# The gated MLP's up-projections as Strassen block products, and its down-projection in pairs of row tiles

## The chip, the core and the metric

The kernel runs on one core of a Trainium2 chip. The metric is device microseconds (us) of one execution. TensorE (PE) does the matmuls and loads their weights (PEld); VectorE (DVE), ScalarE (ACT) and GpSimd (POOL) do the elementwise work; SyncE (SP) and, for a few transfers, ACT and POOL issue DMAs. Each engine takes its instructions in the order in which they stand in its queue; an instruction that waits holds up all behind it. Products accumulate in PSUM, in eight banks of 128 partitions x 512 float32.

## The reference, cut to what matters

One layer of a bidirectional encoder: x is 1024 positions by 1024 model dimensions in float32. Two branches (latent attention and a two-way linear recurrence) are gated, merged by `w_merge` and added to x. What the change touches is what comes then:

```python
x = x + (gates[:, :, 0] * y_a + gates[:, :, 1] * y_b) @ w_merge[l]
h = rms_norm(x, norm_ffn_g[l])
gp = dwconv_centered(h @ w_ffn_gate[l], ffn_conv_w[l], ffn_conv_b[l])   # 3 taps along the positions
x = x + (jax.nn.silu(gp) * (h @ w_ffn_up[l])) @ w_ffn_down[l]
```

`w_ffn_gate` and `w_ffn_up` are 1024 x 2816 and `w_ffn_down` is 2816 x 1024; `rms_norm` divides each position by the root of its mean square and multiplies by the gain `norm_ffn_g`.

## The kernel before, in words

Everything lies transposed: 128 features (or model dimensions) on the partitions, 1024 positions along the free axis, in two halves of 512 (`HT`). A float32 product is made of three passes: each operand is the sum of a high and a low part (`split`: ACT casts the high part, L163; POOL or DVE subtracts it for the low part, L164), and the products high-high, high-low and low-high are added in PSUM. A **pass** here is one matmul of a 128 x 128 weight block with 128 x 512 of the operand.

Phase A is the input projection with its gates; the gates (`gt`) are written to DRAM (`d_gate`). Phase B runs attention and the recurrence, its work on PE ordered by a planner. Phase C, from 1276 us, forms the second branch's product, adds it to the first branch's (`y0`, loaded from DRAM as 512 KB per tile), splits the sum into `yx`, multiplies by `w_merge` (`product(two_, a["w_merge"][j], yx)`), and adds the residual, which gives `x2`, eight tiles j of 128 model dimensions. From each tile come the operands of phase D: `h2h` and `h2l`, the high and low parts of x2 times the gain (L1488 on ACT, L1489 on DVE), and its squares (L1493 on ACT), which POOL adds up (L1494). The residual is not divided by its rms: the product's evacuation multiplies by `rs2`, one over the rms of each position.

Phase D, from 1394 us, is the gated MLP in 22 tiles of 128 features, taken in four groups (`GROUPS`, 6, 6, 5 and 5 tiles). Of each tile, `product` first does the gate half (`w_fg`, 8 row blocks x 2 halves x 3 = 48 passes), then the up half (`w_fu`, 48). DVE evacuates the gate half times `rs2` (L1517), ACT and DVE do the convolution's three taps (L1522, L1523, L1524), ACT applies Silu (L121, in `act`), POOL multiplies by `rs2` (L1527), DVE multiplies with the up half from PSUM (L1528) and splits into `sh` and `sl` (L163, L164). After a group comes its share of the down product: for each of eight output tiles, group size x 2 halves x 3 passes into two banks, which DVE adds onto `x2` (L1535). In the last group each tile is then stored as 512 KB (L1537). The four pairs of banks take turns, so the evacuation of one product lies beside the passes of the next.

SBUF pools lie on two sides. `hp`, on the right, holds the first operands of the projection, and later those of phase D (`place("hh0", ...)` and so on: a tile in the place of an earlier operand). `yq`, `xp2`, `fp` and the weights' pool lie on the left. Weights come in pieces of 128 x 512 float32, 256 KB, through two places (`wraw`, then `whi` and `wlo`), issued by SP.

## Time and profile before

| | us |
|---|---|
| runs | 2135.06, 2125.6, 2127.84 (median 2127.84) |
| span of the profiled execution | 2126.6 |
| PE busy in it | 1958.1 (92%) |
| DVE, ACT, POOL busy | 997.4, 843.1, 871.8 (47%, 40%, 41%) |
| phase C | from 1276 to 1394.2 |
| phase D's matmuls | 1394.2 to 2121.4 |

The profiled execution's span lies 1.2 us under the median of the runs. Several views of the trace are used below. In a table of time windows each row has the window and its length, then the busy time of PE, PEld, DVE, ACT and POOL, each with its count of instructions, then PEclk, the clock that the throttle granted to PE as a share of full speed, then the mean busy share of the 16 DMA engines and GB/s. A row of the groups of instructions names line, engine, operation, output and inputs (`b<-h2h,whi`: bank b from operand h2h and weights whi), shape, count; behind the first bar stand its busy time in total (us) and the mean of one (ns); behind the second the engine's idle time just before these instructions and what ended it. A row of the timeline has start, duration, engine and instruction, with the idle time before it and its releaser in brackets.

### The profile page before, as it was taken

What the parts mean: (1) busy time and instruction counts of PE and PEld (TensorE: products, weight loads), DVE (VectorE), ACT (ScalarE), POOL (GpSimd) and SP (SyncE); (2) the same over time, 40 slices, a digit from 0 to 9 for tenths busy, and PEclk for the clock granted to TensorE, in tenths of its full rate; (3) what the DMA queues carried; (4) which work ended last, traced back from release to release, by engine and by line L of the source; (5) the groups of instructions that cost most, each with busy time, mean ns of one, the idle gap of its engine ahead of it and who ended that gap; (6) DMA issues with size and microseconds to landing.
All of it is one profiled execution on the core that took longest, in us unless ns stands there. A gap on an engine that the chain in (4) does not pass through costs nothing.

```text
span 2126.6 us, 31745 instructions
## 1 busy us (share of the span) xinstructions
PE 1958.1 (92%) x12280; PEld 1507.2 (71%) x12280; DVE 997.4 (47%) x1560; ACT 843.1 (40%) x1459; POOL 871.8 (41%) x763
## 2 busy tenths in 40 slices
PE   7799999899898779888779999999999999999999
...
GB/s 144 34 140 230 145 162 219 104 145 113 98 130 125 78 108 106 104 135 79 100 86 91 205 303 189 50 45 50 43 53 50 50 43 52 50 39 56 50 38 117
DMA packets 212551, 221.09 MB, mean 104 GB/s; under 512 B 114152, under 2 KB 138792, under 8 KB 212400
## 3 DMA queue, kind: packets, MB, share of 16 engines
...
## 4 chain that ended last, share of the span: by engine, by line
PE 51%; DVE 7%; DMA 3%; issue 1%; SPq 1%; POOL 0%; ACT 0%; DVEq 0%; POOLq 0%; ACTq 0%
PE b L251 13%; PE b L248 13%; PE b L249 13%; DMA IN<-dn 2%; DVE Ti L815 2%; DVE tm L811 2%; DVE mx L1151 1%; PE po L1179 1%; PE st L1205 1%; PE po L1181 1%; PE st L1207 1%; PE po L1180 1%; PE st L1206 1%; PE ct L972 1%; PE st L248 1%
## 5 line engine op out<-in xcount | busy, mean ns | idle before, releaser
L164 POOL TENSOR_TENSOR wlo<-wraw,whi 128x512 fp32r<-128x512 f32 x248 | 306.8, 1240 | 792.6 <-ACT whi L163 788.7
L163 ACT CAST whi<-wraw 128x512 fp32r<-128x512 f32 x248 | 145.2, 586 | 652.4 <-PE b L249 462.1
L248 PE MATMUL b<-h2h,whi 128*128 128x512 f32 x704 | 274.3, 390 | 0.0
L249 PE MATMUL b<-h2l,whi 128*128 128x512 f32 x704 | 273.9, 389 | 0.0
L1217 POOL TENSOR_TENSOR pl<-pe,ph 128x512 fp32r<-128x512 f32 x128 | 169.6, 1327 | 131.2 <-ACT ph L1216 128.6
L251 PE MATMUL b<-h2h,wlo 128*128 128x512 f32 x704 | 216.7, 389 | 0.0
L248 PE MATMUL st<-hh,whi 128*128 128x512 f32 x408 | 176.0, 431 | 15.2 <-ACT hh L275 9.0
L249 PE MATMUL st<-hl,whi 128*128 128x512 f32 x408 | 164.7, 404 | 0.5 <-DVE hl L276 0.5
L248 PEld LDWEIGHTS b<-h2h,whi 128*128 128x128 f32 x704 | 132.2, 188 | 27.7 <-issue 0.2
L249 PEld LDWEIGHTS b<-h2l,whi 128*128 128x128 f32 x704 | 132.2, 188 | 27.7 <-issue 0.2
L251 PEld LDWEIGHTS b<-h2h,wlo 128*128 128x128 f32 x704 | 132.2, 188 | 27.5
L251 PE MATMUL st<-hh,wlo 128*128 128x512 f32 x408 | 140.9, 400 | 0.5 <-POOL wlo L164 0.5
L248 PE MATMUL b<-sh,whi 128*128 128x512 f32 x352 | 138.8, 394 | 0.0
L249 PE MATMUL b<-sl,whi 128*128 128x512 f32 x352 | 138.7, 394 | 0.0
L1535 DVE TENSOR_TENSOR x<-b,x 128x1024 f32<-128x1024 f32 x32 | 39.2, 1225 | 197.6 <-PE b L251 197.6
L811 DVE TENSOR_TENSOR tm<-IN,Ti 128x126 f32<-128x126 f32 (+22 forms) x248 | 91.2, 368 | 77.5 <-DMA IN<-dn 71.3
L251 PE MATMUL b<-sh,wlo 128*128 128x512 f32 x352 | 110.4, 394 | 0.0
L248 PEld LDWEIGHTS st<-hh,whi 128*128 128x128 f32 x408 | 79.6, 195 | 43.0 <-issue 9.8
L815 DVE TENSOR_TENSOR Ti<-Ti,tm 128x126 f32<-128x126 f32 (+22 forms) x248 | 104.3, 421 | 6.6
L1517 DVE TENSOR_TENSOR u<-b,rs 128x1024 f32<-128x1024 f32 x22 | 26.9, 1224 | 169.6 <-PE b L251 158.4
L1216 ACT CAST ph<-pe 128x512 fp32r<-128x512 f32 x128 | 79.1, 620 | 64.5 <-PE po L1181 61.3
L980 POOL TENSOR_TENSOR sm<-RR,pcs 64x128 f32<-64x128 f32 x112 | 47.6, 425 | 126.4 <-DVE RR L1002 105.2
...
## 6 DMA issues: line engine op xcount, KB each, us to landing
...
```

Of the source, the lines that this page charges most:

```text
L163: S.copy(hi, x)
L164: (eng or G).tensor_tensor(out=lo, in0=x, in1=hi.bitcast(F32), op=sub)
L248: nc.tensor.matmul(o, wh, xh[:, hs], start=first, stop=False)
L249: nc.tensor.matmul(o, wh, xl[:, hs], start=False, stop=False)
L251: nc.tensor.matmul(o, wl, xh[:, hs], start=False, stop=last)
L811: t = V.tensor_tensor(out=tm[:, 0:nt, 0:nj], in0=IN[:, s, s + 1:32][:, :, None].to_broadcast([128, nt, nj]), in1=Ti[:, s, 0:nj][:, None, : ...
L815: V.tensor_tensor(out=Ti[:, s + 1:32, 0:nj], in0=Ti[:, s + 1:32, 0:nj], in1=tm[:, 0:nt, 0:nj], op=add)
L980: state["pool"] = G.tensor_tensor(out=sm[hs], in0=RR[hs, :, h, 0, :], in1=pcv[hs, i // 4, :, i % 4, None].to_broadcast([64, 2, C]), op=mult)
L1216: S.copy(ph, pe)
L1217: G.tensor_tensor(out=pl, in0=pe, in1=ph.bitcast(F32), op=sub)
L1517: V.tensor_tensor(out=u, in0=pg, in1=rs2, op=mult)
L1535: V.tensor_tensor(out=x2[:, j, :], in0=ps, in1=x2[:, j, :], op=add)
```

## The change

**The operands.** The two up-projections of a feature tile are taken as one product of 2 x 2 blocks. The weights' blocks are A11 and A12 (the halves of `w_fu`'s model dimensions, 0 to 511 and 512 to 1023) and A21 and A22 (of `w_fg`). The operand's are B11 and B12 (dimensions 0 to 511, first and second half of the positions) and B21 and B22 (dimensions 512 to 1023). Strassen's scheme in Winograd's form needs seven products of such blocks where eight stood, here called **one** to **seven**, each of 4 row blocks x 3 = 12 passes into one bank (`quarter`):

| product | weights | operand | bank |
|---|---|---|---|
| one | A11 | B11 | ba |
| two | A12 | B21 | ba, added to one |
| three | s2' = A12 - s2 | B22 | bc, added to five |
| four | A22 | T4 = B21 - T2 | bb, added to six and seven |
| five | s1 = A21 + A22 | T1 = B12 - B11 | bc |
| six | s2 = s1 - A11 | T2 = B11 + T3 | bb |
| seven | A21' = A11 - A21 | T3 = B22 - B12 | bb, added to six |

In the code T1 to T4 are `U1` to `U4`, with tiles named t1h, t1l and so on. T1, T2 and T3 are made in phase C with the tiles j of x2: for j < 4 B11 and T1 (with a subtraction on POOL), for j >= 4 B21, B22, T3 and T2, each with its high and low part. T4 is made at the beginning of phase D, on DVE with ACT's casts (`u2` is its intermediate there). B11, T1, B21 and B22 lie in `hp`, in the places of the earlier h2h and h2l; T2 and T3 lie in a new left-hand pool `bq` (whose places hold y0 and gt before), T4 in `fp`.

**A feature tile.** Four weight blocks are loaded into six places in turn (`raw_`), POOL makes s1, s2, A21' and s2' from them, each is split on ACT and DVE into one of three pairs of places in turn (`parts_`; the down weights' low parts are POOL's). The order on PE is one, six, the down share, five, seven, two, four, three; in the first tile it is one, five, the sums of squares, two, six, seven, four, three. Between them DVE adds bank contents: p1 is a copy of one's bank (ACT), u2 = six + p1, u3 = six and seven + p1; bc + u3 and bb + p1 (after four) give the second and first half of the gate, each multiplied by rs2 into `u`; bc + u2 after three gives the up half's second part. The convolution and Silu follow, then per half the product with the up half in place in PSUM (L1665), and the split into sh (ACT, L1666) and sl (DVE, L1667). The up half is not multiplied by `rs2` any more.

**The residual.** x2 is multiplied after the first tile by the rms itself (`irs`, eight multiplies of 128 x 1024 on POOL, L1670), the down products are added to it, and each half tile is multiplied by rs2 at the very end (DVE, L1697) and stored as 256 KB.

**The down product** goes by pairs of row tiles (2 k blocks) instead of groups of 5 or 6: 16 units of 6 passes, one bank each (three banks `dbank` in turn; the up-projections have five, `fbank`). Half of the units of pair f//2 - 1 stand in tile f, after product six. For even f this pair's second tile is f - 1, the one just before. For the last pair all 16 units follow at the end; the first eight are done with one row tile for all eight banks and then the other.

**Elsewhere.** In phase C y0 and gt lie in `bq`, so the loads of y0 are queued with the places of that pool; the gate stores of j >= 14 in phase A go from ACT's queue instead of POOL's, whose scratch space in SBUF shrinks (`dynamic_dma_scratch_size`). Comments and docstrings fell away.

```diff
-GROUPS = ((0, 6), (6, 12), (12, 17), (17, 22))
...
                 V.tensor_tensor(out=gt, in0=x, in1=rstd[:, hs], op=mult)
-                (G if j >= 14 else nc.sync).dma_start(d_gate[j][:, hs], gt)
+                (S if j >= 14 else nc.sync).dma_start(d_gate[j][:, hs], gt)
...
-        y0 = yp.tile([128, T], F32, tag="y0", name="y0", bufs=2)
...
+        y0 = bq.tile([128, T], F32, tag=f"b{j % 2}", name="y0")
         nc.sync.dma_start(y0, d_y0[j])
-        y = yp.tile([128, T], F32, tag="gt", name="gt", bufs=2)
+        y = bq.tile([128, T], F32, tag=f"b{2 + j % 2}", name="gt")
...
+    B11, U1, B21, B22 = in_hp(0, "b11"), in_hp(2, "t1"), in_hp(4, "b21"), in_hp(6, "b22")
+    U2, U3 = in_pool(bq, "t2", 0), in_pool(bq, "t3", 4)
+    tq = y2.enter_context(pool("tq"))
     acc = place("rstd", "acc2", F32)
+    def scaled(dst, src, g):
+        S.activation(dst[0], src, AF.Copy, scale=g)
+        V.scalar_tensor_tensor(out=dst[1], in0=src, scalar=g, in1=dst[0].bitcast(F32), op0=mult, op1=sub)
     for j in range(8):
         ps, two_ = big4()
         for _ in product(two_, a["w_merge"][j], yx):
             pass
         V.tensor_tensor(out=x2[:, j, :], in0=ps, in1=x2[:, j, :], op=add)
...
+        k, g = j % 4, vc("gffn", j)
+        x1, x2_ = (x2[:, j, hs] for hs in HT)
+        if j < 4:
+            scaled(B11[k], x1, g)
+            d = tq.tile([128, 512], F32, tag="d", name="d")
+            G.tensor_tensor(out=d, in0=x2_, in1=x1, op=sub)
+            scaled(U1[k], d, g)
+        else:
+            g0, x10, x20 = vc("gffn", k), *(x2[:, k, hs] for hs in HT)
+            scaled(B21[k], x1, g)
+            scaled(B22[k], x2_, g)
+            d = tq.tile([128, 512], F32, tag="d", name="b12")
+            S.activation(d, x20, AF.Copy, scale=g0)
+            t3 = tq.tile([128, 512], F32, tag="t3", name="t3f")
+            V.scalar_tensor_tensor(out=t3, in0=x2_, scalar=g, in1=d, op0=mult, op1=sub)
+            split(t3, *U3[k], V)
+            t2 = tq.tile([128, 512], F32, tag="t2", name="t2f")
+            V.scalar_tensor_tensor(out=t2, in0=x10, scalar=g0, in1=t3, op0=mult, op1=add)
+            split(t2, *U2[k], V)
...
     fp = ctx.enter_context(pool("fp"))
...
+    pd = ctx.enter_context(psum("pd"))
+    U4 = in_pool(fp, "t4", 0)
...
+    ones = f5("u3")[:, 0:128]
     G.memset(ones, 1.0)
...
+    for k in range(4):
+        t = f5("u2")
+        V.scalar_tensor_tensor(out=t, in0=x2[:, 4 + k, HT[0]], scalar=vc("gffn", 4 + k), in1=U2[k][0].bitcast(F32), op0=mult, op1=sub)
+        V.tensor_tensor(out=t, in0=t, in1=U2[k][1].bitcast(F32), op=sub)
+        split(t, *U4[k], V)
...
+    def parts_(x, eng):
+        nwt[0] += 1
+        if nwt[0] % 3 == 0:
+            hi, lo = (fp.tile([128, 512], R, tag=t, name=t) for t in ("wh", "wl"))
+        else:
+            hi, lo = (wpool["w"].tile([128, 512], R, tag=t, name=t) for t in ("whi", "wlo"))
+        split(x, hi, lo, eng)
+        return hi, lo
...
+    sh, sl = {}, {}
+    irs = place("rstd", "irs", F32)
+    def norms():
+        for hs in HT:
+            ss = fbank()
+            nc.tensor.matmul(ss, ones, acc[:, hs], start=True, stop=True)
+            act(rs2[:, hs], ss, AF.Ln, scale=1.0 / D, bias=eps)
+        act(irs, rs2, AF.Exp, scale=0.5)
+        act(rs2, rs2, AF.Exp, scale=-0.5)
+    def gate_up(f):
+        def load(w, h):
...
+        A11, A21, A22 = load("w_fu", 0), load("w_fg", 0), load("w_fg", 1)
+        s1, s2 = raw_(), raw_()
+        A12 = load("w_fu", 1)
+        ba, bb, bc = fbank(), fbank(), fbank()
+        p1, u2, u3 = f5("p1"), f5("u2"), f5("u3")
+        def one():
+            quarter(ba, parts_(A11, V), B11, True)
+            S.copy(p1, ba)
+            G.tensor_tensor(out=s1, in0=A21, in1=A22, op=add)
+            G.tensor_tensor(out=s2, in0=s1, in1=A11, op=sub)
+            G.tensor_tensor(out=A21, in0=A11, in1=A21, op=sub)
...
+        def six():
+            quarter(bb, parts_(s2, V), U2, True)
+            V.tensor_tensor(out=u2, in0=bb, in1=p1, op=add)
+            G.tensor_tensor(out=s2, in0=A12, in1=s2, op=sub)
+        def seven():
+            quarter(bb, parts_(A21, V), U3, False)
+            V.tensor_tensor(out=u3, in0=bb, in1=p1, op=add)
+        u = fp.tile([128, T], F32, tag="u", name="u")
+        def u22():
+            V.tensor_tensor(out=u[:, HT[1]], in0=bc, in1=u3, op=add)
+            V.tensor_tensor(out=u[:, HT[1]], in0=u[:, HT[1]], in1=rs2[:, HT[1]], op=mult)
+        if f == 0:
+            one()
+            five()
+            norms()
+            two()
+            six()
+            yield
+            seven()
+            u22()
+            four()
+        else:
+            one()
+            six()
+            yield
+            five()
+            seven()
+            two()
+            u22()
+            four()
+        V.tensor_tensor(out=bb, in0=bb, in1=p1, op=add)
+        V.tensor_tensor(out=u[:, HT[0]], in0=bb, in1=rs2[:, HT[0]], op=mult)
+        three()
+        cv = fp.tile([128, T], F32, tag="cv", name="cv")
+        S.activation(cv, u, AF.Identity, scale=vc("cw1", f), bias=vc("cb", f))
+        V.scalar_tensor_tensor(out=cv[:, 1:], in0=u[:, :-1], scalar=vc("cw0", f), in1=cv[:, 1:], op0=mult, op1=add)
+        V.scalar_tensor_tensor(out=cv[:, :-1], in0=u[:, 1:], scalar=vc("cw2", f), in1=cv[:, :-1], op0=mult, op1=add)
+        V.tensor_tensor(out=bc, in0=bc, in1=u2, op=add)
+        act(cv, cv, AF.Silu)
+        sh[f], sl[f] = (fp.tile([128, T], R, tag=t, name=t, bufs=3) for t in ("sh", "sl"))
+        for b, hs in zip((ba, bc), HT):
+            V.tensor_tensor(out=b, in0=b, in1=cv[:, hs], op=mult)
+            S.copy(sh[f][:, hs], b)
+            V.tensor_tensor(out=sl[f][:, hs], in0=b, in1=sh[f][:, hs].bitcast(F32), op=sub)
+        if f == 0:
+            for j in range(8):
+                G.tensor_tensor(out=x2[:, j, :], in0=x2[:, j, :], in1=irs, op=mult)
+        yield
+    def down(f0, j0, j1, banks=None):
+        last = f0 == NF - 2
+        units = []
+        for j in range(j0, j1, 2):
+            t = wpool["w"].tile([128, 2, 256], F32, tag="wraw", name="wraw")
+            nc.sync.dma_start(t, a["w_fd"][j:j + 2, :, f0 * 128:f0 * 128 + 256].rearrange("j p c -> p j c"))
+            wh, wl = parts_(t.rearrange("p j c -> p (j c)"), G)
+            for i in range(2):
+                for h in range(2):
+                    units.append((j + i, HT[h], wh, wl, 256 * i))
...
+        def out(u, b):
+            j, hs = u[0:2]
+            V.tensor_tensor(out=x2[:, j, hs], in0=b, in1=x2[:, j, hs], op=add)
+            if last:
+                V.tensor_tensor(out=x2[:, j, hs], in0=x2[:, j, hs], in1=rs2[:, hs], op=mult)
+                nc.sync.dma_start(a["outT"][j * 128:(j + 1) * 128, hs], x2[:, j, hs])
+        if banks:
+            for k in range(2):
+                for u, b in zip(units, banks):
+                    mm(u, k, b)
+            for u, b in zip(units, banks):
+                out(u, b)
+        else:
+            for u in units:
+                b = dbank()
+                for k in range(2):
+                    mm(u, k, b)
+                out(u, b)
+    for f in range(NF):
+        part = gate_up(f)
+        next(part)
+        if f > 1:
+            down((f // 2 - 1) * 2, f % 2 * 4, f % 2 * 4 + 4)
+        next(part)
+    down(NF - 2, 0, 4, [fbank() for _ in range(5)] + [dbank() for _ in range(3)])
+    down(NF - 2, 4, 8)
...
+    nc = bacc.Bacc("TRN2", target_bir_lowering=False, num_devices=1, dynamic_dma_scratch_size=1024)
```

**The order of the instructions.** Three places, each as it stands in the engine's queue. First ScalarE, from the last tile of `w_merge` (j = 7) to the first weights of phase D; before:

```order
L1488 ACTIVATE h2h_13588<-x2_12750,vec_63 128x1024
L1493 ACTIVATE rs2_12751<-x2_12750 128x1024
L163 CAST whi_13673<-wraw_13671 128x512
L163 CAST whi_13703<-wraw_13701 128x512
L1488 ACTIVATE h2h_13656<-x2_12750,vec_63 128x1024
L1493 ACTIVATE rs2_12751<-x2_12750 128x1024
L163 CAST whi_13742<-wraw_13740 128x512
```

and after the change (wh_13835 is A12's high part, for product two; whi_13790 is A11's, for product one):

```order
L1496 ACTIVATE b21h_13126<-x2_12750,vec_63 128x512
L1496 ACTIVATE b22h_13130<-x2_12750,vec_63 128x512
L1526 ACTIVATE rs2_12751<-x2_12750 128x1024
L162 CAST t3h1_13138<-t3f_13726 128x512
L162 CAST t2h1_13134<-t2f_13730 128x512
L162 CAST wh_13835<-ra_13781 128x512
L162 CAST whi_13790<-ra_13773 128x512
L162 CAST t4h0_13746<-u2_13752 128x512
```

Before, the casts of phase D's first weights (13673, 13703) stand ahead of the last tile's operand; now product one's weights stand behind all of it, and behind the cast for product two. Second, GpSimd after the sums of squares, in the changed kernel (L1604 to L1606 are s1, s2 and A21', L1623 is s2', first those of tile 0, then tile 1's):

```order
L1527 TENSOR_TENSOR acc2_13144<-acc2_13144,rs2_12751 128x1024 x2
L1545 MEMSET u3_13750 128x128
L1604 TENSOR_TENSOR ra_13779<-ra_13775,ra_13777 128x512
L1605 TENSOR_TENSOR ra_13780<-ra_13779,ra_13773 128x512
L1606 TENSOR_TENSOR ra_13775<-ra_13773,ra_13775 128x512
L1623 TENSOR_TENSOR ra_13780<-ra_13781,ra_13780 128x512
L1670 TENSOR_TENSOR x2_12750<-x2_12750,irs_13772 128x1024 x8
L1604 TENSOR_TENSOR ra_13951<-ra_13947,ra_13949 128x512
L1605 TENSOR_TENSOR ra_13952<-ra_13951,ra_13945 128x512
```

The weight sums of tile 1 stand behind the eight multiplies of x2, where before only splits of weights stood. Third, from the end of tile 9 into tile 10, VectorE in the changed kernel:

```order
L1654 TENSOR_TENSOR fbank_15720<-fbank_15720,p1_15722 128x512
L163 TENSOR_TENSOR wlo_15977<-ra_15946,whi_15976 128x512
L1655 TENSOR_TENSOR u_15725<-fbank_15720,rs2_12751 128x512
L1661 TENSOR_TENSOR fbank_15721<-fbank_15721,u2_15723 128x512
L1659 SCALAR_TENSOR_TENSOR cv_15925<-u_15725,vec_63,cv_15925 128x1023
L1660 SCALAR_TENSOR_TENSOR cv_15925<-u_15725,vec_63,cv_15925 128x1023
L1665 TENSOR_TENSOR fbank_15719<-fbank_15719,cv_15925 128x512
L1665 TENSOR_TENSOR fbank_15721<-fbank_15721,cv_15925 128x512
L1622 TENSOR_TENSOR u2_15953<-fbank_15950,p1_15952 128x512
L163 TENSOR_TENSOR wlo_16071<-ra_15945,whi_16070 128x512
L1667 TENSOR_TENSOR sl_15932<-fbank_15719,sh_15931 128x512
```

and ScalarE (whi_15996 and wh_16002 are down weights, whi_16070 is product five's, L120 is Silu):

```order
L162 CAST whi_15976<-ra_15946 128x512
L1658 ACTIVATE cv_15925<-u_15725,vec_63 128x1024
L162 CAST whi_15996<-wraw_15994 128x512
L162 CAST wh_16002<-wraw_16000 128x512
L1603 COPY p1_15952<-fbank_15949 128x512
L120 ACTIVATE cv_15925<-cv_15925 128x1024
L162 CAST whi_16070<-ra_15945 128x512
L1666 CAST sh_15931<-fbank_15719 128x512
```

and TensorE behind product six of tile 10 (15701, 15702: tile 8's sh and sl; 15931, 15932: tile 9's):

```order
L1574 MATMUL fbank_15950<-t2h1_13134,wlo_15977 128x512
L1689 MATMUL dbank_16006<-sh_15701,whi_15996 128x512
L1690 MATMUL dbank_16006<-sl_15702,whi_15996 128x512
L1691 MATMUL dbank_16006<-sh_15701,wlo_15997 128x512
L1689 MATMUL dbank_16006<-sh_15931,whi_15996 128x512
L1690 MATMUL dbank_16006<-sl_15932,whi_15996 128x512
```

Tile 9's `sl` stands on VectorE behind two steps of tile 10, its Silu on ScalarE behind two casts and a copy of tile 10, and the down product reads it in its fifth pass.

92 lines of the change are left out of this document (45 added, 47 removed).

## The prediction

> **What bounds the kernel now.** I read the table of time windows first, for the stage that the change rewrites (phase D, from 1394 us), then the groups of TensorE (PE) there.
>
> ```profile
> 1276.00:1394.00 118.00, 118.00 (x510) 95.30 (x510) 40.72 (x38) 40.64 (x48) 42.70 (x28) 1.00 0.32 112
> 1394.00:1594.00 200.00, 200.00 (x871) 163.13 (x870) 49.46 (x40) 48.75 (x64) 64.16 (x47) 1.00 0.15 47
> 1594.00:1990.00 396.00, 396.00 (x1733) 324.60 (x1732) 96.47 (x78) 85.91 (x119) 123.41 (x95) 1.00 0.15 49
> L248 PE MATMUL b<-h2h,whi 128*128 128x512 f32 x704 | 274.3, 390 | 0.0
> L251 PE MATMUL b<-sh,wlo 128*128 128x512 f32 x352 | 110.4, 394 | 0.0
> L192 PE MATMUL b<-acc,ones 128*128 128x512 f32 x4 | 1.9, 592 | 0.0
> ```
>
> In the first three rows PE is busy in every microsecond at full clock; VectorE (DVE), ScalarE (ACT) and GpSimd (POOL) are a quarter to a third busy. The group rows end in 0.0: PE never idles there. So phase D lasts as long as its passes (a pass is one 128x512 matmul), and a pass removed is worth its spacing, as long as nothing makes PE wait. The spacing is read from the timeline, two rows of each kind:
>
> ```profile
> 1500.29 0.62 PE L251 MATMUL b<-h2h,wlo 128*128 128x512 f32 x2
> 1513.89 0.62 PE L251 MATMUL b<-h2h,wlo 128*128 128x512 f32 x2
> 2095.54 0.63 PE L251 MATMUL b<-sh,wlo 128*128 128x512 f32 x2
> 2106.74 0.63 PE L251 MATMUL b<-sh,wlo 128*128 128x512 f32 x2
> ```
>
> Between the first two lie ten rounds of 6 passes: 13.60/60 = 0.2267 us. Between the others eight rounds: 11.20/48 = 0.2333. Operands in the right-hand pool are read at the first rate, those in left-hand pools at the second. Phase D is 2112 x 0.2267 + 1056 x 0.2333 + 1.9 = 727 us, and 1394.2 to 2121.4 is 727.
>
> **The gain.** A feature tile needs 96 gate and up passes now (21.76 us) and 84 then: seven products of 12. B11, T1, B21 and B22 lie where h2h lies, 48 x 0.2267; T2, T3 and T4 lie on the left, 36 x 0.2333; together 19.28. That saves 2.48 x 22 = **54.6 us**. Bounds: 47.6 if all 84 run at 0.2333; 66.8 if the left-hand operands of all 1848 new passes and of the 1056 unchanged down passes come to 0.2267 in their new places (5.2 and 7.0 more). I take the sides as they are.
>
> **What the other engines do for it.** Durations for the pieces, from the groups:
>
> ```profile
> L1269 DVE TENSOR_TENSOR gt<-b,gt 128x512 f32<-128x512 f32 x16 | 10.3, 684 | 7.4 <-PE b L251 4.1 <-ACT gt L121 3.2
> L164 DVE TENSOR_TENSOR sl<-sg,sh 128x1024 fp32r<-128x1024 f32 x22 | 26.9, 1225 | 24.5 <-ACT sh L163 24.5
> L1523 DVE SCALAR_TENSOR_TENSOR cv<-u,vec,cv 128x1023 f32<-128x1023 f32 x22 | 28.2, 1284 | 28.9 <-ACT cv L1522 28.9
> L1489 DVE SCALAR_TENSOR_TENSOR h2l<-x,vec,h2h 128x1024 fp32r<-128x1024 f32 x8 | 10.3, 1285 | 9.7 <-ACT h2h L1488 9.7
> L276 DVE SCALAR_TENSOR_TENSOR hl<-xt,vec,hh 128x1024 fp32r<-128x1024 f32 x8 | 21.5, 2720 | 6.4 <-ACT hh L275 6.4
> L163 ACT CAST whi<-wraw 128x512 fp32r<-128x512 f32 x216 | 134.0, 620 | 595.8 <-PE b L249 421.0 <-issue 92.9 <-PE po L249 33.9
> L921 ACT COPY BT<-sc 128x512 f32<-128x512 f32 x32 | 18.7, 585 | 15.9 <-PE sc L920 15.4
> L1522 ACT ACTIVATE cv<-u,vec 128x1024 f32<-128x1024 f32 x22 | 27.4, 1245 | 22.0 <-DVE u L1517 22.0
> L121 ACT ACTIVATE sg<-cv 128x1024 f32<-128x1024 f32 x22 | 23.3, 1057 | 2.8 <-DVE cv L1524 2.8
> L1493 ACT ACTIVATE rs<-x 128x1024 f32<-128x1024 f32 x7 | 7.3, 1042 | 0.0
> L1527 POOL TENSOR_TENSOR sg<-sg,rs 128x1024 f32<-128x1024 f32 x22 | 52.7, 2396 | 2.3 <-ACT sg L121 2.3
> 1394.72 1.29 POOL L164 TENSOR_TENSOR wlo<-wraw,whi 128x512 fp32r<-128x512 f32 x1 [4.11 <-ACT whi L163]
> 20.73 6.63 POOL L283 TENSOR_TENSOR xacc<-xacc,xt 128x1024 f32<-128x1024 f32 x2
> 21.66 6.78 DVE L276 SCALAR_TENSOR_TENSOR hl<-xt,vec,hh 128x1024 fp32r<-128x1024 f32 x2
> ```
>
> So 0.69 for a DVE piece of 512 that reads PSUM, 0.62 (half of 1.225) in SBUF, 0.62 for an ACT cast, 1.29 for POOL's. A tile then gives DVE about 18 PSUM pieces, 8 SBUF pieces and two conv steps, 20 us in 30.5 us of PE; ACT 10; POOL six pieces, 8. The removed POOL multiply (2.40 a tile) is more than repaid. No engine becomes the bound; the four loads of 256 KB a tile leave DMA at about its 0.15. What costs is order: three weight places in turn, and short products (2.7 us) between dependent steps.
>
> The last two rows are one more price: POOL and DVE, both on SBUF operands, take 3.3 and 3.4 us a piece together, where POOL's 128x1024 piece takes 2.40 and DVE's 1.29 alone. They take turns. The Trainium skill ("SBUF — State Buffer", Who interferes with whom) says that a DVE instruction with two SBUF inputs and a reading GpSimd instruction exclude each other, whole instructions long; the two rows agree.
>
> **The wait of every second tile.** In even tiles from 2 to 20 the down product's first unit needs, as its fifth pass, the low part of the tile just before (sl). Clock 0 is the end of that tile's product "four". PE goes on with three, one, six (2.72, 2.72, 2.80) and reaches that pass at 9.0. DVE and ACT, in the order shown above: four's evacuation, six's split and u's first half to 2.1; the add to the third bank waits for three, 2.75 to 3.4; conv steps (1.28, 1.33 by their rows) to 6.1; on ACT, two down splits and the copy p1 stand ahead of Silu, and the second split and p1 wait for product one (5.4), so Silu runs 6.7 to 7.8; two multiplies to 9.2, u2 to 9.9, five's split to 10.5, sl to 11.2. PE waits **2.2 us**. With turns on the port, s2 on POOL holds back six's split, and the first down split falls between the conv steps: Silu 8.0 to 9.1, sl at 12.5, a wait of 3.5. I take 2.8, by the 2720 ns of L276, which shows the turns: 10 x 2.8 = **28** (22 to 35). Odd tiles read older sl and wait for nothing; the third bank's readers are through before five writes there.
>
> **The clock.** What a gap costs beyond itself:
>
> ```profile
> 1268.30:1271.70 3.40, 1.76 (x6) 1.16 (x7) 3.37 (x4) 2.05 (x3) 1.89 (x2) 1.00 0.86 323
> 1271.70:1275.10 3.40, 3.40 (x9) 2.60 (x8) 1.71 (x2) 1.21 (x2) 1.62 (x1) 0.51 0.94 337
> 1275.10:1278.50 3.40, 3.40 (x16) 2.80 (x15) 0.79 (x2) 1.61 (x2) 0.57 (x1) 0.99 1.02 398
> ```
>
> PE idle 1.64 of 3.40 us is followed by 3.4 us at half clock, 9 matmuls started where 16 fit: 7 x 0.233 = 1.6 us. A gap of 2.8, cut in two by a single pass, holds some 2.4 idle; seven of ten should fall so in a window: **11** (0 to 16).
>
> The Trainium skill ("TensorE: Matmul & The Clock Gate", Why this matters for your kernels) lets the clock fall for idle gaps above about 3 us. By it this term would be 0; the rows here show the fall after 1.64 us idle.
>
> **Entering phase D.** Clock 0 is the end of the last w_merge product. Before, h2h's last tile was needed only eight rounds later. Now the cast of the first weights (A11) stands on ACT behind the last tile's two casts, square, t3, t2 and one more weight cast: DVE's evacuation to 1.25, then 0.62 x 2 + 1.04 + 0.62 x 4 = 4.8, so the high part is there at 6.1; DVE brings the low part behind t2's rest and two steps of T4, at 8.1. Wait 7.9; with turns against POOL's sum of squares (2.4) and three weight sums, 13.7. In tile 0, seven and four wait for u2 and u3 with no down product between: 1.3 and 0.9. Then the eight multiplies of x2 by the rms, 8 x 2.40 = 19.2, stand on POOL ahead of tile 1's s1 and s2: from rms ready they take 19.2 + 2.6 + 1.3 for the split, against 17 us of PE's work left plus its 2.2 of waits: 5.9. Together 15.9 (to 26 with turns, which also stretch the eight); I take **19**, and **4** for two or three windows of half clock.
>
> **The end.** Unit 3 of the last down group takes the bank that tile 21's first half still holds (to 9.1), while PE is at 4.7: 4.4 us. Then each of 16 units needs two DVE steps (0.69 + 0.62) and DVE sets the end: first unit at 13.5, plus 16 x 1.31 = 34.5, against 30.2 for PE as before; the halved store gives back about 1:
>
> ```profile
> 2120.77 0.63 PE L251 MATMUL b<-sh,wlo 128*128 128x512 f32 x2
> 2121.43 1.22 DVE L1535 TENSOR_TENSOR x<-b,x 128x1024 f32<-128x1024 f32 x1 [5.77 <-PE b L251]
> 2122.68 0.33 SPq L1537 DMA_DIRECT2D outT<-x  x1
> ```
>
> PE's 30.2 is 25.0 (product three, 96 passes) and the 5.2 from 2121.4 to the span's end. With half clock in the gap I take **8.5** (6 to 11).
>
> **Before phase C.** Two y0 loads of 512 KB move on SP's queue behind gate loads and ahead of w_o weights, where PE already waits on weights (the 1.76 row; 323 GB/s): 1 MB/323 GB/s is 3.2 if all of it delays them, 0 if none; **1.5**. Four gate stores go from POOL's queue to ACT's, among attention casts: nothing, or some tenths.
>
> **Sum.** 28 + 11 + 19 + 4 + 8.5 + 1.5 = 72 lost against 54.6: +17.4 on the span of 2126.6 is 2144. The span lies 1.2 under the median of the runs, 2127.84; so **2145 us**, 0.8% slower. The measurement tells about 0.5% (10.6 us) from no change.
>
> **Rivals.**
> *Faster:* the ports don't exclude each other for these short pieces, the clock holds, and the new places are read at 0.2267: 66.8 - 15.9 - 22 - 7.7 - 1.5 = 20 gained, 2108. It decides once the even wait is 2.2 or less and spacing 0.2267. For it: L1269's pieces keep 0.68. Against: L276. Chance 0.21.
> *Break-even:* spacing by sides, no turns, some half clock: 15.9 + 3 + 22 + 8 + 7.7 + 1.5 = 58 against 54.6: 2131. Chance 0.25.
> *The clock holds:* as forecast but without the 11: 2134. For it, gaps are under a whole 3.4 us window; against, the 0.51 row. Chance 0.09.
> *Full price:* turns everywhere: 35 + 16 + 26 + 5 + 10 + 3 = 95 against 54.6: 2168. Chance 0.12.
> *Forecast:* 0.33, its own range 2136 to 2155.
> That the products aren't fewer is excluded: the queue holds 84 passes a tile.
>
> Faster takes 0.21 and a hundredth of break-even; no change takes 0.20 of break-even, 0.07 of the clock's, 0.06 of the forecast; the rest, 0.45, is slower. The range 2112 to 2162 leaves out half of the outer rivals.
>
> **What would show it.** Right: PE idle before L1690 for a DVE releaser, 2 to 3.5 us, ten times; PE idle of 8 us or more before the first L1574 and again in tile 1, released by ACT behind POOL L1605; half clock in phase D, where there was none; L1697 closing the kernel with DVE busy. Wrong: PE idle under 25 us in phase D, spacing of t2, t3 and t4 at 0.227, conv steps at 1.28 beside POOL's splits.

## The result

The changed kernel takes **2162.14 us** (median of 4 runs, 2158.32 to 2164.57); the kernel before takes 2127.97 us beside it. The ratio is 1.0152, 95% interval 1.0131 to 1.0173: **1.5% slower**, 34 us. Forecast were 2145 us and slower; the time lies a tenth of a microsecond above the upper end of the stated range (2162) and well above the forecast's own one (2136 to 2155). Two executions far off all others (6151.07 us in run 8, 2687.63 us of the kernel before) are left out of the medians and ratios below.

The windows of the profiled execution after the change (its span is 2162.8 us; columns as in the prediction):

```profile
1276.00:1394.00 118.00, 111.75 (x472) 89.52 (x471) 66.07 (x57) 48.34 (x62) 48.20 (x30) 0.97 0.42 145
1410.00:1440.00 30.00, 16.66 (x55) 12.09 (x56) 26.99 (x26) 14.74 (x22) 17.03 (x9) 0.75 0.11 35
1594.00:1990.00 396.00, 385.57 (x1615) 309.15 (x1614) 255.48 (x341) 114.51 (x170) 113.96 (x75) 0.97 0.16 49
```

Where every microsecond of 1594 to 1990 was PE's at clock 1.00, PE is now idle for 10.4 us of 396 and the clock is 0.97; DVE's share rose from 24% to 65%. Between 1410 and 1440 PE does 55 passes in 30 us. The longest waits of PE from 1394 us to the end (us in total, times, longest):

```profile
PE dbank L1690 <- DVE sl L1667: 12.7, 10, 1.3
PE fbank L1574 <- ACT wh L162: 8.1, 1, 8.1
PE fbank L1574 <- DVE wlo L163: 6.2, 1, 6.2
PE fbank L1574 <- ACT whi L162: 5.7, 1, 5.7
PE fbank L1689 <- DVE sl L1667: 5.5, 1, 5.5
PE dbank L1689 <- ACT sh L1666: 4.7, 10, 0.5
PE fbank L1574 <- DVE u L1622: 2.9, 1, 2.9
```

Before, PE had no idle time there at all. These rows are the prediction's places: the even tiles' sl (ten times), the entry (A11's two parts), tile 1 behind the multiplies of x2 (8.1), tile 0's u2, and the end.

**The account of the two profiled executions.** Their spans differ by 36.2 us. I took the starts of phase D's 2908 PE rows, each as a distance from the row before, and sorted the distances: below 0.3 us they are spacing (0.2312 in the mean), with an idle time they are a wait, the rest is half clock. The border is the first w_merge pass, ahead of which PE does the same passes in both programs:

```profile
1304.64 0.39 PE L248 MATMUL b<-yh,whi 128*128 128x512 f32 x1
```

in the kernel before, and after the change

```profile
1318.79 0.39 PE L247 MATMUL b<-yh,whi 128*128 128x512 f32 x1
```

| term | forecast | measured |
|---|---|---|
| fewer passes | -54.6 | 2908 x 0.2312 - 727.0 = -54.7 |
| even tiles' waits | 28 | 21.7 (10 x 2.17) |
| half clock in these tiles | 11 | 13.2 |
| entry, with tiles 0 and 1 | 19 | 24.9 |
| half clock there | 4 | 7.4 |
| end, with its half clock | 8.5 | 9.6 |
| ahead of w_merge | 1.5 | 14.15 |
| sum | +17.4 | +36.3 |

Two of the rows for half clock hold 1.0 us each that is none: the four passes over the squares, which took as long before (it is in the gain, too), and in the even tiles the first pass behind each long wait, 0.33 us. The end has 0.4 us behind PE's last pass. Phase D lost 22 us where 16 were forecast; the rest of the miss lies ahead of it.

### The profile page after: what moved, and what is told of

Its sections match the earlier page's. It is cut to its first block, busy times and chain, and to the rows that moved or that the text cites. A ratio compares the mean times of both kernels' runs of the same rounds, so it can differ in the third digit from the quotient of the medians.

```text
span 2162.8 us, 31814 instructions
## 1 busy us (share of the span) xinstructions
PE 1942.0 (90%) x12016; PEld 1475.6 (68%) x12016; DVE 1341.1 (62%) x2086; ACT 904.7 (42%) x1575; POOL 875.3 (40%) x729
## 4 chain that ended last, share of the span: by engine, by line
PE 44%; DVE 13%; DMA 4%; issue 1%; ACT 1%; SPq 1%; POOL 0%; DVEq 0%; ACTq 0%; POOLq 0%
PE fbank L1574 17%; PE dbank L1690 4%; PE dbank L1691 4%; PE dbank L1689 3%; DMA IN<-dn 2%; DVE Ti L814 2%; DVE tm L810 2%; PE b L250 2%; PE b L248 2%; PE b L247 2%; DVE cv L1660 1%; PE po L1178 1%; DVE mx L1150 1%; DVE cv L1659 1%; PE st L1204 1%
## 5 line engine op out<-in xcount | busy, mean ns | idle before, releaser
L163 POOL TENSOR_TENSOR wlo<-wraw,whi 128x512 fp32r<-128x512 f32 x118 | 176.0, 1492 | 326.6 <-ACT whi L162 305.4
L1695 DVE TENSOR_TENSOR x<-dbank,x 128x512 f32<-128x512 f32 x171 | 116.8, 688 | 81.5 <-PE dbank L1691 79.7
L1604 POOL TENSOR_TENSOR ra<-ra 128x512 f32<-128x512 f32 x22 | 29.5, 1341 | 332.4 <-DVE wlo L163 332.4
L162 ACT CAST whi<-wraw 128x512 fp32r<-128x512 f32 x118 | 72.7, 616 | 135.1 <-PE b L248 42.8
L163 DVE TENSOR_TENSOR wlo<-ra,whi 128x512 fp32r<-128x512 f32 x110 | 84.2, 766 | 40.2 <-ACT whi L162 40.2
L120 ACT ACTIVATE pe<-st 128x512 f32<-128x512 f32 x128 | 76.2, 597 | 42.0 <-PE st L1206 34.0
L250 PEld LDWEIGHTS st<-hh,wlo 128*128 128x128 f32 x408 | 79.8, 196 | 20.0 <-POOL wlo L163 1.5
L1150 DVE TENSOR_REDUCE mx<-st 128x1 f32<-128x512 f32 x112 | 73.3, 682 | 30.4 <-PE st L1149 30.1
L248 PEld LDWEIGHTS st<-hl,whi 128*128 128x128 f32 x408 | 80.0, 196 | 16.7 <-DVE hl L275 1.4
L1690 PE MATMUL dbank<-sl,whi 128*128 128x512 f32 x174 | 75.0, 431 | 12.7 <-DVE sl L1667 12.7
L1689 PE MATMUL dbank<-sh,whi 128*128 128x512 f32 x174 | 74.8, 430 | 5.5 <-ACT sh L1666 4.7
```

The lines of the kernel that those rows point to most:

```text
L162: S.copy(hi, x)
L163: (eng or G).tensor_tensor(out=lo, in0=x, in1=hi.bitcast(F32), op=sub)
L248: nc.tensor.matmul(o, wh, xl[:, hs], start=False, stop=False)
L250: nc.tensor.matmul(o, wl, xh[:, hs], start=False, stop=last)
L1689: nc.tensor.matmul(b, wh[:, ws], xh[:, hs], start=(k == 0), stop=False)
L1690: nc.tensor.matmul(b, wh[:, ws], xl[:, hs], start=False, stop=False)
```

## The experiments

"Phase D" below is the time from the end of the last w_merge pass to the end of PE's last one in the profiled execution: 727.0 us before, 748.7 after. It is free of what phases A to C do, which scatters (below). The kernel before was timed beside each group of runs: 2128.89 (26 runs), 2130.14 (22) and 2130.09 (17).

**1. The even tiles' wait and the clock.** Only the order of passes in the down product changes:

```diff
-            for u in units:
-                b = dbank()
-                for k in range(2):
-                    mm(u, k, b)
-                out(u, b)
+            n = 3 if j0 == 0 and not last else 0
+            bs = [dbank() for _ in range(n)]
+            for k in range(2):
+                for u, b in zip(units, bs):
+                    mm(u, k, b)
+            for u, b in zip(units, bs):
+                out(u, b)
+            for u in units[n:]: ...
```

> The changed kernel with the first three down units of each even tile done with the older row tile for all three banks first, and the newer after it; sl is then read six passes (1.4 us) later. The wait of 2.17 us of PE time in each even tile shrinks to 0.8: 14 us. Theory 'clock by windows' (half clock follows a window that holds over 1.5 us of idle): the 13 us of half clock in these tiles go too: 2162 - 27 = 2135, no half-clock window between 1500 and 2110 us. Rival 'any gap': a gap of any size costs its half clock: 2148.

Measured: 2129.71 us (10 runs; ratio to before 1.0009, 0.999 to 1.0029), so 32.4 us less than the change. Phase D fell to 721.5, by 27.2; the forecast of the window theory was 27. The other 5 us lie ahead of phase D, which this edit does not touch: scatter (run 8). Of this kernel, the wait in the list of waits, and a window:

```profile
PE dbank L1690 <- DVE sl L1667: 6.1, 10, 0.6
1594.00:1990.00 396.00, 391.76 (x1687) 315.68 (x1686) 268.95 (x359) 120.41 (x179) 117.69 (x77) 1.00 0.17 52
```

A wait of 0.6 us costs no clock (1.00). In the changed kernel the same place cost clock in eight of ten tiles; it is read from the distance of one even tile's first waiting pass to the next's:

```profile
1486.96 0.50 PE L1689 MATMUL dbank<-sh,whi 128*128 128x512 f32 x1 [0.47 <-ACT sh L1666]
1550.30 0.50 PE L1689 MATMUL dbank<-sh,whi 128*128 128x512 f32 x1 [0.46 <-ACT sh L1666]
...
1808.25 0.50 PE L1689 MATMUL dbank<-sh,whi 128*128 128x512 f32 x1 [0.46 <-ACT sh L1666]
1873.12 0.50 PE L1689 MATMUL dbank<-sh,whi 128*128 128x512 f32 x1 [0.47 <-ACT sh L1666]
```

63.34 us where the clock held, 64.87 where it did not: 1.53 us for gaps of the same size. What differs is their place. The half-clock stretches give the border of the windows; here are the windows of the gaps of tiles 2 and 6, and the one behind the latter:

```profile
1486.66:1490.08 3.42, 1.85 (x7) 1.32 (x8) 3.19 (x6) 0.83 (x2) 0.00 (x0) 1.00 0.49 141
1612.96:1616.37 3.41, 1.67 (x6) 1.03 (x6) 3.18 (x6) 1.17 (x2) 0.00 (x0) 1.00 0.41 111
1616.37:1619.79 3.42, 3.42 (x9) 2.69 (x9) 1.18 (x2) 0.00 (x0) 0.00 (x0) 0.50 0.13 48
```

With 1.57 us idle in a window the clock held, with 1.74 it fell (in tile 4 the border parts the gaps, 1.19 and 0.55, and it held). The Trainium skill ("TensorE: Matmul & The Clock Gate", Why this matters for your kernels) lets the clock fall for gaps above about 3 us; these, of 1.27 and 0.46 us with one pass between, made it fall eight times, and the trace decides. From tile 6 on the trace has 61.44 us at full clock and 3.41 at half in turn, together nineteen windows: an even tile then meets the windows where the one before met them, and falls again.

**2. What is late in the even tiles.** The changed kernel's own timeline shows it, at the end of tile 9.

```profile
1800.02 0.68 DVE L1655 TENSOR_TENSOR u<-fbank,rs 128x512 f32<-128x512 f32 x1
1802.18 1.27 DVE L1659 SCALAR_TENSOR_TENSOR cv<-u,vec,cv 128x1023 f32<-128x1023 f32 x1
1802.57 2.04 POOL L163 TENSOR_TENSOR wlo<-wraw,whi 128x512 fp32r<-128x512 f32 x1 [1.08 <-ACT whi L162]
1803.49 2.20 DVE L1660 SCALAR_TENSOR_TENSOR cv<-u,vec,cv 128x1023 f32<-128x1023 f32 x1
1805.79 1.06 ACT L120 ACTIVATE cv<-cv 128x1024 f32<-128x1024 f32 x1 [0.54 <-DVE cv L1660]
1808.09 0.68 DVE L1622 TENSOR_TENSOR u<-fbank,p 128x512 f32<-128x512 f32 x1
1808.68 0.68 DVE L163 TENSOR_TENSOR wlo<-ra,whi 128x512 fp32r<-128x512 f32 x1
1809.28 1.28 DVE L1667 TENSOR_TENSOR sl<-fbank,sh 128x512 fp32r<-128x512 f32 x2
1810.02 0.50 PE L1690 MATMUL dbank<-sl,whi 128*128 128x512 f32 x1 [1.27 <-DVE sl L1667]
```

The two conv steps are the same work on the same operands. The first takes 1.27; the second, which begins while POOL splits the down weights, 2.20, and POOL's split 2.04 instead of 1.29. So they do take turns, at this one place of the chain; six's split and the steps around it ran untouched. Then u2 and five's split of the next tile (1.2 us) stand ahead of sl, as the order had it. Product four ends at 1798.8: Silu runs from 7.0 to 8.1 and sl's first half is there at 11.2.

**3. The end.** Four of tile 21's eight down units go behind tile 21's last product (with the order of run 1):

```diff
+        if f == NF - 1:
+            down(NF - 4, 4, 6)
+        elif f > 1:
             down((f // 2 - 1) * 2, f % 2 * 4, f % 2 * 4 + 4)
         next(part)
+    down(NF - 4, 6, 8)
     down(NF - 2, 0, 4, [fbank() ...
```

> The changed kernel with the even tiles' first three down units by row tiles, as in the run before, and half of tile 21's down share (4 units, 5.6 us of PE) put behind tile 21's last product instead of into it. Prediction's theory: PE's wait of 5.5 us at the end is for the banks that tile 21 still holds; with 5.6 us of other passes ahead it goes, with a half-clock window: 2130 - 5.5 - 2 = 2122.5. Rival: VectorE's 16 units of 1.3 us set the end (its queue, not PE): 2129.

Measured: 2126.74 us (10 runs; ratio 0.998, 0.9963 to 0.9997), 3 under run 1, and phase D 715.4, by 6.1 under it. The wait for the banks fell from 5.5 to 0.8 us:

```profile
PE fbank L1689 <- DVE sl L1667: 0.8, 1, 0.8
```

DVE kept up with its 16 units: 5.5 us lie behind PE's last pass, as in the change. The rival falls, and with it the half of the prediction's working by which DVE's units set the end.

**4. The multiplies of x2.** Four go behind tile 1's weight sums on POOL, four behind tile 2's down splits (`behind` sets the order of two instructions in one queue; `sums` and `parted_` hold the last weight sum and split):

```diff
-        if f == 0:
-            for j in range(8):
-                G.tensor_tensor(out=x2[:, j, :], in0=x2[:, j, :], in1=irs, op=mult)
+        if f in (1, 2):
+            x = (sums if f == 1 else parted_)[0]
+            for j in range(4 * f - 4, 4 * f):
+                behind(G.tensor_tensor(...), x)
```

> The changed kernel with the eight multiplies of x2 by the rms moved on GpSimd: four behind tile 1's weight sums, four behind tile 2's down splits. Prediction's theory: they hold up tile 1's s1 and s2; PE's wait of 8.1 us before product six of tile 1 goes, and with it a half-clock window or two: 2162 - 8 to 11 = 2151 to 2154. Rival 'backlog': VectorE is late there anyway (T4, u2, u3), and the wait turns up at the next product: 2159 or more.

Measured: 2157.36 us (4 runs; 1.0134, 1.0115 to 1.0152), 4.8 less than the change, phase D 744.9, 3.8 less. Both theories hold half. The 8.1 us before product six are gone, but product seven of tile 1 (T3) then waits for something else on DVE. From the timelines:

```profile
1439.90 11.90 POOL L1723 TENSOR_TENSOR x<-x,irs 128x1024 f32<-128x1024 f32 x4
1446.17 3.42 DVE L1665 SCALAR_TENSOR_TENSOR cv<-u,vec,cv 128x1023 f32<-128x1023 f32 x1
1453.47 0.68 DVE L1627 TENSOR_TENSOR u<-fbank,p 128x512 f32<-128x512 f32 x1
1454.29 0.76 PE L1574 MATMUL fbank<-t3h,whi 128*128 128x512 f32 x1 [5.42 <-ACT sh L1671]
```

Beside the four multiplies, DVE's two conv steps of tile 0 and two splits take 2.78, 2.90, 3.42 and 2.84 us, 11.9 in all, where such steps take 1.27 and 0.68 alone. Tile 0's products with Silu follow, and only then u2 of tile 1, which must read product six's bank before seven adds to it. The view names ACT's sh, which ended beside u2 (1454.17 and 1454.15); but seven's bank had been in use since six, so no bank of tile 0 holds it up. In later tiles a down share stands between six and seven as well and hides u2; tile 1 has none.

**5. The first products made early.** A11 and s1 of tile 0 are loaded and split between the last w_merge product and its evacuation; T4 is made after product six's emission:

```diff
+        if j == 7:
+            e11 = pieces(early(..., a["w_fu"][0][:, HT[0]]))
+            ...
+            G.tensor_tensor(out=e22, in0=e21, in1=e22, op=add)
+            es1 = pieces(e22)
         V.tensor_tensor(out=x2[:, j, :], in0=ps, in1=x2[:, j, :], op=add)
```

> The changed kernel with the first two products of phase D made ready early: A11 and s1 of tile 0 are loaded and split ahead of the last w_merge tile's operands on ScalarE and VectorE, and T4 is made behind product six's split instead of ahead of tile 0. Prediction's theory: PE waits there only because A11's casts stand behind that chain; products one and five (5.6 us) then run at once, PE waits for product two's split for some 3 us, and some of the 7 us of half clock go: 2162 - 8 to 14 = 2148 to 2154. Rival 'work': VectorE has 12 us of work there in any order, and PE waits as long, only one product later: 2159 or more.

Measured: 2165.83 us (4 runs; 1.0168, 1.0141 to 1.0195): no gain, phase D 755.3, 6.6 longer. The first waits went as the theory has it, from 5.7 + 6.2 to 1.4 + 1.6 us. But POOL came to the multiplies of x2 earlier: two of them slipped ahead of product six's weight sum, and beside the other six, DVE's pieces took four times as long. From the timelines of this kernel, POOL and DVE:

```profile
1418.11 1.71 POOL L1621 TENSOR_TENSOR ra<-ra 128x512 f32<-128x512 f32 x1
1421.46 16.59 POOL L1687 TENSOR_TENSOR x<-x,irs 128x1024 f32<-128x1024 f32 x6
1424.83 2.71 DVE L1564 SCALAR_TENSOR_TENSOR t4f<-x,vec,t2h 128x512 f32<-128x512 f32 x1
1427.58 2.71 DVE L1565 TENSOR_TENSOR t4f<-t4f,t2l 128x512 f32<-128x512 f32 x1
1430.21 2.83 DVE L163 TENSOR_TENSOR wlo<-ra,whi 128x512 fp32r<-128x512 f32 x1
1433.10 0.80 PE L1590 MATMUL fbank<-t2h,wlo 128*128 128x512 f32 x1 [10.30 <-DVE wlo L163]
```

DVE pieces of 0.68 to 0.75 us take 2.7 to 2.8: each gets its turn only when a POOL piece of 2.77 (16.59/6) ends. The rival "work" has a share, as steps of T4 still stand ahead of six's split on DVE; but what makes them long is not how much DVE has to do, but beside what. The Trainium skill ("SBUF — State Buffer", Who interferes with whom) has such an exclusion by whole instructions for a DVE instruction with two SBUF inputs; here it shows. Steps with one operand in PSUM keep their time: in the change L1654 and L1655 take 0.69 each at 1448.67 and 1449.40, while POOL's eight multiplies run.

**6. All mendings together**, and besides them sl placed ahead of u2 and of five's split on DVE (from tile 1 on), and tile 0 in the down product's three banks (for the wait of run 4, which was not for a bank; no run shows that this does anything):

```diff
-        ba, bb, bc = fbank(), fbank(), fbank()
+        ba, bb, bc = (fbank() if f else dbank() for _ in range(3))
-            V.tensor_tensor(out=u2, in0=bb, in1=p1, op=add)
+            i = V.tensor_tensor(out=u2, in0=bb, in1=p1, op=add)
+            if f:
+                behind(i, lastsl[0], "after the low part of the tile before")
...
+            w = parts_(s1, V) if f else es1
+            if f:
+                behind(parted_[0], lastsl[0], "after the low part of the tile before")
+            quarter(bc, w, U1, True)
```

> All of the mendings at once on the changed kernel: even tiles' down units by row tiles, sl ahead of u2 and of five's split on VectorE, the early first products, the multiplies of x2 spread, the end's four units moved, and tile 0's products in the down product's three banks so that tile 1 does not wait for tile 0's banks. If each loss is what the prediction said it is, they add up: 2162 - 32 (measured) - 11 - 5 (measured) - 5 (tile 1's remaining wait) - 7.5 = 2101. Rival: VectorE is the bound behind them (1341 us busy in the page, two thirds of phase D), and what one mending gains another loses: 2115 or more.

Measured: 2118.94 us (6 runs; ratio 0.9941, 0.9922 to 0.9959): faster than before, yet above the 2101 of the sum. Phase D is 708.6. In the steady tiles PE no longer waits, with DVE two thirds busy:

```profile
1594.00:1990.00 396.00, 395.38 (x1703) 318.66 (x1702) 271.45 (x361) 122.13 (x181) 119.57 (x78) 1.00 0.17 52
PE fbank L1590 <- DVE wlo L163: 8.4, 1, 8.4
```

So DVE is not the bound. The second row is again tile 1: five's split stands behind sl there, without a down share to hide it, and ahead of sl two conv steps take 2.76 and 3.31 us beside POOL's multiplies.

**7. Tile 1 once more.** The order of run 6 applies from tile 2 on, and the multiplies of x2 stand behind tile 2's weight sums (s2 and A21') and its down splits; the two were not run apart.

```diff
-            if f:
+            if f > 1:
                 behind(parted_[0], lastsl[0], ...)
+            if f == 2:
+                scale(0, 4, [i, m])
```

> The run with all mendings, with two of them mended in turn: in tile 1, which has no down share between products six and five, five's split is no longer put behind tile 0's sl (PE waited 8.35 us there), and the multiplies of x2 go behind tile 2's weight sums and down splits instead of beside tile 0's convolution, whose two steps took 2.76 and 3.31 us there instead of 1.28. Theory: that wait and a half-clock window go: 2119 - 12 = 2107. Rival: VectorE's other work of tile 1 keeps five's split late, and the multiplies stretch tile 1's steps instead: 2115 or more.

Measured: 2114.78 us (6 runs; ratio 0.9939, 0.9926 to 0.9953). Phase D is 701.4, 7.2 less. Of the time no gain is shown: the median is 4 us lower, but the ratios, 0.9941 and 0.9939, are the same. The 8.4 went; 4.0 came back in tile 2, whose first down split now stands behind four multiplies and a sum:

```profile
PE dbank L1723 <- POOL wlo L163: 4.0, 1, 4.0
```

**8. What lies ahead of phase D.** Three runs take the parts of the change that touch phases A to C and put them alone into the kernel before; one takes a part out of the mended kernel. First, the gate stores with the smaller scratch, then the scratch by itself:

```diff
-                (G if j >= 14 else nc.sync).dma_start(d_gate[j][:, hs], gt)
+                (S if j >= 14 else nc.sync).dma_start(d_gate[j][:, hs], gt)
-    nc = bacc.Bacc(..., num_devices=1)
+    nc = bacc.Bacc(..., num_devices=1, dynamic_dma_scratch_size=1024)
```

> The kernel before with one part of the change alone: the gate stores of j >= 14 go from ScalarE's queue and GpSimd's scratch is cut to 1024. Of the 36 us that the profiled change lost, 10 lie ahead of phase C, where the prediction gave this part nothing. Prediction's theory: no change, 2128 (within 2 us), and PE at the same place in phase C within 2 us of before. Rival 'queue': the stores among ScalarE's casts, or the shifted left-hand pools, cost those 10 us: 2138, with a drift that is there in every execution. Rival 'windows': the 10 us are half-clock windows that fall differently from execution to execution: the times scatter by some 5 us around 2128 to 2133, and the profile shows more or fewer half-clock windows in phases A and B with the same waits.

> The kernel before with GpSimd's scratch cut to 1024 and its gate stores left on GpSimd's queue. Theory 'queue': what cost 8 us in the first run is the stores among ScalarE's casts; here nothing changes: 2129. Rival 'scratch': the pools lie 15 KB lower, or GpSimd waits for scratch: 2137.

Measured: with the stores on ACT's queue 2136.01 us (8 runs; ratio 1.0038, 1.0024 to 1.0052), 5 to 11 us slower, which the prediction had at nothing. The scratch alone: 2129.39 (11 runs; ratio 1.0000, 0.9984 to 1.0017). So, by subtraction, it is the queue, not the pools' places. Then the places of y0 and gt alone (`yp` closed with phase C against `bq` opened ahead of `yq`):

```diff
+    bq = ctx.enter_context(pool("bq"))
     y2 = ExitStack()
     yq = y2.enter_context(pool("yq"))
-        y0 = yp.tile([128, T], F32, tag="y0", name="y0", bufs=2)
+        y0 = bq.tile([128, T], F32, tag=f"b{j % 2}", name="y0")
```

> The kernel before with y0 and gt of phase C in a pool of its own ahead of yq, as the change has them, and nothing else of the change (the freed places take the first two kinds of phase D's intermediates). The first two y0 loads then stand on SP's queue between the gate loads, ahead of the w_o weights, as in the change. Prediction's theory: 1.5 us, from 0 to 3.2: 2129.5. Rival 'whole load': the w_o weights wait for both loads and a half-clock window more: 4 us, 2132, with PE's wait for the w_o cast at 6 us instead of 2.5.

Measured: 2135.45 us (12 runs; ratio 1.0028, 1.0018 to 1.0038), 4 to 8 us slower, where the prediction had 3.2 at most. PE's wait for the w_o weights, of the kernel before, of this run, and after the change:

```profile
PE b L248 <- ACT whi L163: 2.5, 1, 2.5
```

```profile
PE b L248 <- ACT whi L163: 4.6, 1, 4.6
```

```profile
PE b L247 <- ACT whi L162: 6.0, 1, 6.0
```

In the run with the stores alone, whose loads are those of before, this wait is 4.1, so it is not the loads' alone.

Between 1268 and 1275 us, where this wait lies, PE's lag against the kernel before grows by 3.3 us in the run of the y0 places, by 2.4 in that of the stores, by nothing in the scratch run, and by 3.5 to 4.6 (4.6 in the change) in the eight kernels with both parts: the change and seven runs built on it. The rest cannot be told so from one execution. The two ratios, 8.1 + 6.0 us, make the 14.15 of the account, but that is chance. The first w_merge pass starts at 1304.6 and 1305.7 in the two profiles with neither part (before, and the scratch run), at 1311.6 and 1313.4 with one of them, and with both between 1307.4 and 1318.8, mean 1312.4. The medians say the same: less phase D's time, they leave 1401.9 to 1403.1 us with neither part, 1408.5 and 1409.1 with one, and 1408.2 to 1413.4, mean 1411.4, with both (the change, runs 1 and 3 to 7). Together the two cost some 9 us, little more than either alone; the rest of the 14.15 is scatter. Nor does the trace show the stores' cost where they stand (645 to 664 us): that run's lag is 0.1 us at 650 and 2.0 at 700, and the 5.1 that it gains from 750 to 900 are 5.0 and 5.9 in the runs of the scratch and of the y0 places.

Up to 1152 us the same instructions drift by 1 to 10 us against the kernel before, and the change's own profile is the farthest. The places of this drift are half-clock windows: where the change first drifts, between 238 and 255 us, both kernels wait the same 1.8 us, and the clock then stays at half for one window before, for three after (10.24 us). Of the kernel before, then of the change:

```profile
238.00:241.40 3.40, 1.61 (x4) 0.29 (x2) 3.40 (x4) 1.67 (x3) 2.67 (x3) 0.93 0.60 193
241.40:244.80 3.40, 3.40 (x8) 2.12 (x8) 2.24 (x3) 0.69 (x1) 2.11 (x1) 0.57 0.64 257
244.80:248.20 3.40, 3.40 (x11) 1.57 (x10) 0.00 (x0) 1.42 (x3) 0.93 (x1) 1.00 0.31 129
```

```profile
238.00:241.40 3.40, 1.61 (x5) 0.48 (x3) 3.40 (x5) 1.80 (x4) 2.87 (x2) 0.91 0.59 192
241.40:244.80 3.40, 3.40 (x7) 1.82 (x6) 2.51 (x4) 0.81 (x2) 2.16 (x1) 0.50 0.58 233
244.80:248.20 3.40, 3.40 (x6) 1.59 (x6) 0.00 (x0) 0.69 (x1) 0.00 (x0) 0.50 0.37 154
```

Last, the stores back on GpSimd's queue in the kernel of run 7, with the small scratch:

> The same, with the gate stores of j >= 14 on GpSimd's queue again, while its scratch stays at 1024. If the 8 us of the first run lie in the stores' queue: 8 us under the run beside it (2099). If they lie in the shifted pools or the small scratch: the same as that, or slower, where GpSimd has to wait for scratch.

Measured: 2113.3 us (6 runs; ratio 0.993, 0.9908 to 0.9951), 1.5 under run 7, phase D 701.3 as there. The difference of the ratios is 0.0009 with some 0.0025 of uncertainty: neither nothing nor the most of 8 us is excluded, though all 8 are not borne out. By which way the stores cost what they cost in the kernel before, and whether they cost it in this one, **stays open**.

**9. The other queue, and later loads.** To the kernel of run 6: the gate stores on SP, and the residual's loads in phase C three or more steps later.

```diff
-                (S if j >= 14 else nc.sync).dma_start(d_gate[j][:, hs], gt)
+                nc.sync.dma_start(d_gate[j][:, hs], gt)
```

> As the run with all mendings, and besides it what lies ahead of phase D: the four gate stores on SyncE's queue, and the residual's eight loads of 512 KB three or more steps later, behind the w_o weights. If the stores on ScalarE's queue cost their 8 us there, and the loads of phase C their 4 to 6: 12 us under that run. If the shifted pools cost the 8 us (they stay as they are): 4 us under it. If the stores hold up loads behind them on SyncE: no gain.

Measured: 2132.28 us (12 runs; ratio 1.0004, 0.9988 to 1.0019), 13 us slower than run 6. From 661 us on PE waits 16.2 us in one piece that run 6 does not have (run 6 has one of 9.2 between 600 and 720 us that is missing here), and SP waits 7.2 us, in four pieces, for the gates it has to store; that the one makes the other is not shown. In phase C the later loads shortened PE's wait for w_o by nearly 3 us and made a new one of 2.2 us at the first `yx`. The two parts were not run apart.

**10. The side of the weights.** In the kernel of run 1, the three places of weights are dealt out one product later (`nraw, nwt = [0], [1]`); the left-hand place (wh, wl) then goes to the first down split, seven and three, instead of one, two and the second down split. The other two places are on the right: the weights' pool is a right-hand one, and not on the left as the words on the kernel before have it.

> The kernel with the down units by row tiles, with the three places of weights dealt out one product later, so that products seven and three and the first down split take the left-hand place (wh, wl) instead of one, two and the second down split. If the spacing of passes goes by the side of the moving operand alone: the same for each operand as before (t3 0.2334, b11 0.2287, sh beside wh 0.2273). If it goes by whether weights and operand lie on the same side: t3 falls to 0.227 with weights on the left, b22 rises towards 0.233, and b11 and b21 come to 0.2303 or less with weights on the right.

Measured: 2126.57 us, one execution. Product seven (T3, on the left) from its first pass to the next product's first, with weights on the right in run 1 and on the left here:

```profile
1705.97 0.39 PE L1574 MATMUL fbank<-t3h,whi 128*128 128x512 f32 x1
...
1708.77 0.40 PE L1574 MATMUL fbank<-b21h,wh 128*128 128x512 f32 x1
```

```profile
1705.66 0.39 PE L1574 MATMUL fbank<-t3h,wh 128*128 128x512 f32 x1
...
1708.39 0.39 PE L1574 MATMUL fbank<-b21h,whi 128*128 128x512 f32 x1
```

2.80/12 = 0.2333 and 2.73/12 = 0.2275 us. Over all tiles of steady state the means go as the second reading says: T3 from 0.2333 to 0.2276, B22 (right) from 0.2301 to 0.2331 as its weights go left, B21 (right) from 0.2331 to 0.2302 as its weights come right. B11 does not follow it: on the right, it takes 0.2290 with weights on the left and 0.2285 with weights on the right.

## Why the prediction came out as it did

**The gain** was right in size: 54.6 forecast, 54.7 measured. Its parts were not: by "Operands in the right-hand pool are read at the first rate", B11, T1, B21 and B22 should take 0.2267, and took 0.2290 to 0.2331 (B21), while half of the down passes, given 0.2333, took 0.228. Mostly it is the pair of operand and weights that counts, and before the change all weights of phase D lay on the right. That the errors nearly cancel (0.2 us a tile one way, 0.13 the other) was luck.

**The even tiles.** Place, releaser and number (ten) as forecast. The size was 2.17, under the lower bound's 2.2: I let the turns delay both six's split and a conv step, and only the second conv step had one. In the term's sum 21.7 for 28.

**The clock** was right in its rule: run 1 shows that the idle part of a window decides. Its size, 13.2 for 11 (8 x 1.53 = 12.2 without the passes behind the waits), was luck. The gaps held 1.74 us idle and not 2.4, within a stretch of 2.24 us, nearly all of which has to fall into one window of 3.41: an estimate from these figures is four tiles in ten. Eight came because the period with one fall is a whole number of windows.

**The entry** was right in its first wait (5.7 + 6.2 = 11.9, between the 7.9 and 13.7 given) and in tile 0's second (0.9); tile 0's first took 2.9 for 1.3. In tile 1 I had 5.9 and measured 8.1: the multiplies stretch with the turns, to 2.64 each (21.11/8) where I used 2.40. The whole, 24.9, lies above the 19 taken and within the 26 given. Run 4 shows what the working left out: the same turns stretch DVE's steps beside the multiplies, and u2 of tile 1 stands behind these.

**The end** came near, 9.6 for 8.5, and run 3 shows that the bank's wait was its cause. The other half of the working, DVE's 16 units as what sets the end, was wrong: 5.5 us lie behind PE's last pass, against 5.2 before. Its sum does not give 8.5 either: 34.5 - 30.2 - 1 is 3.3, and one window of half clock is some 1.6.

**The step that failed** is "Before phase C": "1.5" for the loads of y0, and for the gate stores "nothing, or some tenths". In their place the profiled execution has 14.15 us and the medians some 9. For the loads I divided the bytes by the rate and took half; PE's wait for w_o grew by 2.1 us in the run of the loads and by 3.5 in the change, and with the half clock behind it 3.3 and 4.6 us were lost there. For the stores I looked at what they move and not at what stands behind them in ACT's queue, where a store waits for DVE's gate and the attention's casts wait with it. That is argued from the queue's order, not shown. With 14 in place of 1.5 the sum is 2157 for the profiled execution; the other 6 are the entry, the clock and the end, less the even tiles. Of the 17 us by which the median lies above the forecast, some 6 are phase D and the end, some 7 are this step, and the rest is scatter.

Of the rivals, "faster" and "break-even" fell with the waits; "the clock holds" is excluded by the 0.97 of the window; "full price" (2168) came nearest in time, but by another sum: its turns everywhere did not come.

## The version that beats both

The kernels of runs 6 and 7 are faster than the kernel before; the best is that of run 7 with the stores on GpSimd's queue, 2113.3 us against 2130.09, ratio 0.993 (0.9908 to 0.9951). Of the 54 us that the fewer passes are worth it keeps 26 in phase D (701.3 for 727.0); PE still waits 15 us in its first 70 us.
